# Another order of the expert blocks, and the loop over further blocks and the loads of the sums moved ahead of the last down products

## The chip, the cores and the metric

The kernel runs on one core of one Trainium2 chip. The metric is the device time of one execution in microseconds (us). Three timed executions of the kernel before gave 1248.77, 1251.58 and 1253.98 us; the median, 1251.58 us, is the time that counts.

## The reference, cut to what matters

One transformer block. A mixer (a gated delta net and a gated linear recurrence, both in two directions, over 256 context and 1024 latent tokens) and a first norm come first; the change does not touch them. What follows is a mixture of experts over the 1024 latent tokens h:

```python
combine = jnp.einsum('tk,tke->te', top_w, jax.nn.one_hot(expert_id, N_EXPERTS))   # 2 of 32 experts for each token
a = jnp.einsum('td,edf->tef', h, w_gate[sl])      # 1024 -> 256
b = jnp.einsum('td,edf->tef', h, w_up[sl])
part = jnp.einsum('tef,efd->td', jax.nn.silu(a) * b * combine[:, sl, None], w_down[sl])   # 256 -> 1024
...
x = post_norm(DEEP_ALPHA * x + gt2_l * f_l, ln_g[l, 1], ln_b[l, 1])
```

All 32 experts are used, so the weights of all of them are read: 2 MB of gate and up weights and 1 MB of down weights for each, in f32.

## The kernel before, in words

**Blocks.** The 2048 pairs of token and expert are packed into 22 blocks of 128 rows. Experts are ranked by how many tokens chose them, and `SHAPE` says which ranks share a block: blocks 0 to 2 belong to rank 0, blocks 3 to 9 to ranks 1 to 7, and blocks 10 to 21 hold pieces of several ranks (21 holds ranks 28 to 31, 20 holds ranks 21, 22, 26 and 27, the others two ranks each). `ORDER` lists the blocks in the order in which they are computed. Below, a block is called by its place in that order, so place 0 is block 21 in both kernels.

**A block.** `gather` (L1496, GpSimd) fetches its 128 token rows from DRAM, `transpose` (L1505, 8 TensorE transposes) turns them, `up` (L1529) multiplies them by the gate and up weights, contraction tile by contraction tile: tiles 0 to 3 need the first of the two loads of an expert's up weights, tiles 4 to 7 the second. Then come the SiLU (L1531, ScalarE) and the product (L1532, VectorE), `turn` (L1538, two transposes, and the copy L1540), and `down` (L1553 and the scaling L1554). `scatter` (L1565, GpSimd) adds the 128 rows to the sums `acc` in DRAM. In a block of several ranks a token can stand twice; `alike` and `join` (L1576, L1588) add such rows up first, on TensorE. The last two places (`LATE`) are not scattered: their products stay in SBUF (`keep`, L1556 and L1557) and TensorE adds them at the end.

**Weights.** `ahead` hands out 18 places of 8 KB per partition (`UNITS`); one expert takes two for up and one for down, so six experts fit. It issues loads on SyncE's queue (L1396 up, L1402 down) in the order in which `ORDER` first uses the experts. A load waits until its place is free and, by `behind` with `DEPTH` 2, until the load before last has landed, so at most two are under way. The `ahead` call that follows the first three gathers passes `after`: the first load that this call issues also waits for that gather.

**Order of the work.** A scheduler lays out each engine's instructions at compile time, from priorities in program order and a timing model. So instructions can stand on an engine in another order than in the code. The loop over further blocks (L1660, for pairs that found no room in the 22 blocks) has a count read at run time. For the inputs here the count is zero and the body is skipped, but each engine must still reach the loop, wait there for everything that the other engines and the DMA queues were given ahead of it, and branch past it.

**The end.** After the loop come the loads of ln_g and ln_b (L1697, L1698) and of the eight tiles of sums `xs` (L1705, 0.5 MB each). `total` then adds, tile by tile, the kept products of the last two places (L1723) and, for six of the eight tiles, the sums by an identity matrix (L1725); for tiles 0 and 3 VectorE adds them (L1743). The norm (ScalarE L1747 and L1748, a chain on GpSimd, VectorE L1751 and L1752) and the stores (L1755) close the kernel.

Of the kernel before, what the change touches and what calls it, by code (L numbers as in the profile page):

```python
# [9 lines left out]
F32 = mybir.dt.float32  # L10
F32R = mybir.dt.float32r
I32 = mybir.dt.int32
# [18 lines left out]
         + [[(2, 64), (20, 64)], [(11, 64), (19, 64)], [(12, 64), (18, 64)], [(14, 64), (17, 64)], [(15, 64), (16, 64)]]  # L31
         + [[(21, 32), (22, 32), (26, 32), (27, 32)], [(r, 32) for r in range(28, 32)]])

ORDER = [21, 4, 15, 5, 19, 16, 1, 11, 17, 0, 18, 2, 20, 3, 6, 12, 10, 8, 7, 13, 14, 9]


def plan():
# [52 lines left out]
def hybrid_block(ctx, tc, x, c, ctx_in, c_ctx, w_ada, b_ada, w_in, conv_qkv_w, dn_a_log, dn_dt_bias, dn_onorm_w,  # L90
# [1181 lines left out]
    def split(slot, n, name, s0, T_=T_, ge=None):  # L1272

        ge = T_([P, 2, n, 32], name + "ge") if ge is None else ge
        sk, ski, hii = T_([P, 2, n], name + "sk"), T_([P, 2, n], name + "ski", I32), T_([P, 2, n], name + "hii", I32)
        slo, shi = T_([P, 2, n], name + "slo"), T_([P, 2, n], name + "shi")
        V.tensor_tensor(ge, slot[:, None].to_broadcast([P, 2, n, 32]), Of[:, :, s0:s0 + n], op=ALU.mult)
        V.tensor_reduce(sk, ge, axis=AX.X, op=ALU.add)
        V.tensor_copy(ski, sk)
        V.tensor_scalar(hii, ski, 7, None, op0=ALU.arith_shift_right)  # L1280
        V.tensor_copy(shi, hii)
        V.tensor_scalar(ski, ski, 127, None, op0=ALU.bitwise_and)
        V.tensor_copy(slo, ski)
        return slo, shi
# [93 lines left out]
    def place(i, shape):  # L1378

        return pool_of(i).tile(shape, F32, name=f"u{i}", tag=f"u{i}")  # L1380
# [9 lines left out]
    def load_w(e, places, after=None):  # L1390

        ws = []
        src = w_up[bass.ds(e, 1)].rearrange("o p (k f) -> p (o k) f", k=KT)
        for q, i in enumerate(places):
            w = place(i, [P, 4, 512])
            behind(nc.sync.dma_start(w, src[:, 4 * q:4 * q + 4, :]), None if q else after)  # L1396
            ws.append(w)
        return ws

    def load_d(e, places, after=None):  # L1400
        w = place(places[0], [P, 2, D])
        behind(nc.sync.dma_start(w, w_down[bass.ds(e, 1)].rearrange("o p (k f) -> p (o k) f", k=2)), after)  # L1402
        return w
# [10 lines left out]
    def ahead(done, done_d, after=None):  # L1414

        for h, k in zip(held, (done, done_d)):
            for r in sorted(h, key=lambda r: uses[r][-1]):
                if uses[r][-1] <= k:
                    free.extend(h.pop(r))
        if not known:  # L1420
            return
        for r in uses:
            for ws, h, load, n in ((W, held[0], load_w, 2), (Wd, held[1], load_d, 1)):
                if r not in ws:
                    if len(free) < n or any(pool_of(i) is None for i in free[:n]):
# [171 lines left out]
    def count_over():  # L1597
# [8 lines left out]
        V.tensor_scalar(ov, ov, 128.0, 128.0 * NBLK, op0=ALU.mult, op1=ALU.add)  # L1606
        V.tensor_tensor(ov, ov, kv[:, 3, :], op=ALU.subtract)

    blocks, keeps = [], []

    def make(i):
# [7 lines left out]

    for i in range(3):  # L1620
        make(i)
    ahead(-1, -1, after=blocks[2].got)
    blocks[0].transpose()
    for i in range(NBLK + 1):
        if i < NBLK:
# [16 lines left out]
            blocks[i - 1].join()  # L1642
        if i == 2:
            count_over()


    osm = sb.tile([P, D], F32, name="osm", tag="xg1")
    used = [0]

    def O_(shape, name, dt=F32):  # L1650
        n = int(np.prod(shape[1:]))
        o = osm[0:shape[0], used[0]:used[0] + n]
        used[0] += n
        o = o if dt == F32 else o.bitcast(dt)
        return o if len(shape) == 2 else o.rearrange("p (a b) -> p a b", b=shape[-1]) if len(shape) == 3 else o.rearrange("p (a b c) -> p a b c", b=shape[2], c=shape[3])

    nov = nc.values_load(novi[0:1, 0:1], min_val=0, max_val=48)
    jb = O_([P, 1], "jb")
    V.memset(jb, 0.0)
    with tc.For_i(0, nov, 1):  # L1660
        jn = O_([P, 1], "jn")
        V.tensor_scalar_add(jn, jb, float(NBLK))
        osp = sb.tile([P, 4, 8, 32], F32, name="osp", tag="xg2")
        oslot, oge = osp[:, 0], osp[:, 1]
        V.tensor_tensor(oge, pos, bc(kv[:, 3, :], 8), op=ALU.is_lt)
        V.tensor_tensor(oslot, pos, bc(ov, 8), op=ALU.add)
        V.scalar_tensor_tensor(oslot, oge, BIG, oslot, op0=ALU.mult, op1=ALU.add)
        oslo, oshi = split(oslot, 8, "ov", 0, O_, osp[:, 2:4])
        bv = O_([P, 2, 8, 2], "obv")
        V.tensor_scalar(oge[:, 0:2, 0:8], oshi, jn, None, op0=ALU.is_equal)  # L1670
        for i in range(2):
            V.tensor_tensor(bv[:, :, :, i], oge[:, 0:2, 0:8], valw[:, i], op=ALU.mult)
        pt = psm.tile([P, 512], F32, name="ptab", tag="ptab")
        for k in range(2):
            alo = sb.tile([P, 8, P], F32, name="xT", tag="xT", bufs=2)
            V.tensor_tensor(alo, io128[:, None, :].to_broadcast([P, 8, P]), oslo[:, k, :, None].to_broadcast([P, 8, P]), op=ALU.is_equal)
            for s in range(8):
                nc.tensor.matmul(pt[:, 0:2], alo[:, s, :], bv[:, k, s, :], start=k == s == 0, stop=k == 1 and s == 7)
        ori, ow = rows_of(pt, 1, "ob")
        le = O_([1, 32], "le")  # L1680
        V.tensor_scalar(le, oin[0:1, :], jb[0:1, :], None, op0=ALU.is_le)
        ef = O_([1, 1], "ef")
        V.tensor_reduce(ef, le, axis=AX.X, op=ALU.add)
        ei = O_([1, 1], "ei", I32)
        V.tensor_copy(ei, ef)
        V.tensor_scalar_add(jb, jb, 1.0)
        e = nc.sync.value_load(ei[0:1, 0:1], min_val=0, max_val=31)
        one = Block(0, [(0, 0, P)], ori, ori, ow)
        one.gather()
        one.transpose()  # L1690
        one.up([load_w(e, (0, 1))])
        one.turn()
        one.down([load_d(e, (2,))])
# [100 lines left out]
```

## Time and profile before

| what | value |
|---|---|
| median of 3 timed runs | 1251.58 us (1248.77 to 1253.98) |
| profiled execution: own time, span | 1239.28 us, 1237.5 us |
| TensorE busy, share of the span | 1122.5 us, 91% |
| mean granted TensorE clock | 0.936 |
| DMA moved | 250.65 MB, mean 203 GB/s |
| loads of expert weights | 96 of 1 MB, the first issued at 805.2 us |
| first up products / last down products / end of the span | 883.4 / 1195.5 / 1237.5 us |

A page of the profile gives the busy time of each engine, the span in 40 slices with TensorE's granted clock and the DMA engines' busy share, the groups of instructions, and the DMA issues. The trace answers finer questions: busy time in any window, an engine's instructions in order of time, and what ended an engine's idle time.

### The profile page before, as it was taken

What the parts mean: (1) busy time and instruction counts of PE and PEld (TensorE: products, weight loads), DVE (VectorE), ACT (ScalarE), POOL (GpSimd) and SP (SyncE); (2) the same over time, 40 slices, a digit from 0 to 9 for tenths busy, and PEclk for the clock granted to TensorE, in tenths of its full rate; (3) what the DMA queues carried; (4) which work ended last, traced back from release to release, by engine and by line L of the source; (5) the groups of instructions that cost most, each with busy time, mean ns of one, the idle gap of its engine ahead of it and who ended that gap; (6) DMA issues with size and microseconds to landing.
All of it is one profiled execution on the core that took longest, in us unless ns stands there. A gap on an engine that the chain in (4) does not pass through costs nothing. (4 is left out here: it accounts for less than half of the span.)

```text
span 1237.5 us, 18636 instructions
## 1 busy us (share of the span) xinstructions
PE 1122.5 (91%) x6828; PEld 712.1 (58%) x6828; DVE 689.3 (56%) x1676; ACT 432.7 (35%) x776; POOL 397.0 (32%) x507
## 2 busy tenths in 40 slices
PE   5799998998999989987899999887699998899985
PEld 2357776776867767655677776666343333234343
DVE  3727569568595785785535867756323223123337
ACT  0534513324231544892221345534112222112213
POOL 1511405214243142342860057563112212111106
PEclk7799999898999999988899999986699999899988
DMA  9503453563545423005888355498799999999956
GB/s 335 179 24 121 146 135 111 140 177 109 150 124 155 113 79 85 1 35 184 263 288 252 133 166 185 154 329 300 264 330 317 338 345 342 340 315 336 309 197 195
DMA packets 145605, 250.65 MB, mean 203 GB/s; under 512 B 35627, under 2 KB 97255, under 8 KB 133224
## 3 DMA queue, kind: packets, MB, share of 16 engines
q1 hardware_dynamic: 132688, 215.94, 52.6%
q0 software_dynamic: 6048, 16.01, 5.3%
q10 hardware_dynamic: 6776, 17.49, 3.7%
q8 instruction: 54, 0.88, 0.3%
q14 instruction: 39, 0.32, 0.1%
HBM read 205.34 MB, written 50.09 MB: 206 GB/s over the span
## 5 line engine op out<-in xcount | busy, mean ns | idle before, releaser
L405 PE MATMUL pj<-hhi,whi 128*128 128x512 f32 (+1 forms) x480 | 189.0, 394 | 4.9 <-ACT s L441 2.8
L406 PE MATMUL pj<-hlo,whi 128*128 128x512 f32 (+1 forms) x480 | 185.8, 387 | 0.0
L407 PE MATMUL pj<-hhi,wlo 128*128 128x512 f32 (+1 forms) x480 | 184.6, 385 | 0.0
L1529 PE MATMUL pu<-u,xT 128*32 128x512 f32 (+2 forms) x768 | 172.5, 624 | 5.5 <-DMA u<-in_w_up_dram 5.0
L405 PEld LDWEIGHTS pj<-hhi,whi 128*128 128x128 f32 x480 | 92.8, 193 | 50.2 <-issue 19.1
L1529 PEld LDWEIGHTS pu<-u,xT 128*32 128x32 f32 (+2 forms) x768 | 54.2, 136 | 92.9 <-issue 78.1
L407 PEld LDWEIGHTS pj<-hhi,wlo 128*128 128x128 f32 x480 | 92.6, 193 | 20.9 <-issue 5.7
L406 PEld LDWEIGHTS pj<-hlo,whi 128*128 128x128 f32 x480 | 92.9, 194 | 19.3 <-issue 5.3
L401 POOL TENSOR_TENSOR wlo<-wraw,whi 128x1024 fp32r<-128x1024 f32 x21 | 53.5, 2546 | 154.2 <-ACT whi L400 117.8
L1553 PE MATMUL py<-u,hT 128*32 128x512 f32 (+2 forms) x384 | 83.6, 614 | 2.0 <-ACT hT L1540 2.0
L1496 POOL DMA_INDIRECT xg<-h2d,tbri x22 | 22.9, 1041 | 170.0 <-PE pf L1505 129.3
L621 DVE TENSOR_TENSOR s<-s,s 80x31 f32<-80x31 f32 (+15 forms) x124 | 65.1, 525 | 19.6 <-DMA s<-ad 10.1
L436 DVE SCALAR_TENSOR_TENSOR cv<-pj,par,cv 128x504 f32<-128x504 f32 (+3 forms) x96 | 63.9, 669 | 11.1 <-ACT cv L424 10.0
L1509 ACT ACTIVATE xT<-pf,mod 128x128 f32<-128x128 f32 x88 | 34.2, 456 | 93.9 <-PE pf L1505 93.7
L1532 DVE TENSOR_TENSOR hid<-hid,pu 128x256 f32<-128x256 f32 x22 | 9.3, 421 | 95.5 <-ACT hid L1531 95.5
L623 DVE TENSOR_TENSOR s<-s,s 80x31 f32<-80x31 f32 (+15 forms) x124 | 58.5, 472 | 2.3
L1554 DVE SCALAR_TENSOR_TENSOR y<-py,tbw,gt 128x512 f32<-128x512 f32 x44 | 33.0, 750 | 47.8 <-PE py L1553 47.5
L405 PE MATMUL pf<-whi,yh 128*128 128x512 f32 x128 | 55.2, 431 | 3.7 <-ACT yh L1029 2.6
L1553 PEld LDWEIGHTS py<-u,hT 128*32 128x32 f32 (+2 forms) x384 | 27.1, 135 | 50.3 <-issue 46.4
L407 PE MATMUL pf<-whi,yl 128*128 128x512 f32 x128 | 53.3, 416 | 0.6 <-POOL yl L1030 0.6
L406 PE MATMUL pf<-wlo,yh 128*128 128x512 f32 x128 | 53.1, 415 | 0.0
L1174 DVE SCALAR_TENSOR_TENSOR S<-S,dec,p 128x128 f32<-128x128 f32 x144 | 40.6, 341 | 21.2 <-PE p L1167 20.9
(514 smaller groups left out, 2147.0 us busy)
## 6 DMA issues: line engine op xcount, KB each, us to landing
u<-in_w_up_dram SPq DMA_DIRECT2D x64, 1024.0 KB, 7.4
u<-in_w_down_dram SPq DMA_DIRECT2D x32, 1024.0 KB, 8.7
st<-sp SPq DMA_DIRECT2D x52, 384.0 KB, 4.9
wraw<-in_w_ada_dram SPq DMA_DIRECT2D x32, 512.0 KB, 3.8
wraw<-in_w_in_dram SPq DMA_DIRECT2D x24, 512.0 KB, 5.9
wada<-in_w_ada_dram SPq DMA_DIRECT2D x4, 2048.0 KB, 8.2
sp<-t SPq DMA_DIRECT2D x12, 512.0 KB, 4.3
wor<-in_w_out_dram SPq DMA_DIRECT2D x8, 512.0 KB, 5.9
```

The source lines that it names most:

```text
L401: (nc.vector if i in PA["LOV"] else nc.gpsimd).tensor_tensor(lo, raw, hi.bitcast(F32), op=ALU.subtract)
L405: nc.tensor.matmul(o, lh, rh, start=start, stop=False)
L406: nc.tensor.matmul(o, lh, rl, start=False, stop=False)
L407: nc.tensor.matmul(o, ll, rh, start=False, stop=stop)
L436: nc.vector.scalar_tensor_tensor(yo, xi, w(j), yo, op0=ALU.mult, op1=ALU.add)
L621: nc.vector.tensor_tensor(t_, sa[:, j + 1:32, j:j + 1].to_broadcast([80, n, j + 1]), T[:, j:j + 1, 0:j + 1].to_broadcast([80, n, j + 1]), ...
L623: nc.vector.tensor_tensor(T[:, j + 1:32, 0:j + 1], T[:, j + 1:32, 0:j + 1], t_, op=ALU.subtract)
L1174: nc.vector.scalar_tensor_tensor(s2[:, d, :], S[h][:, d, :], gl[:, (t + d) % 2, m, d, h:h + 1], p3[d][:, h, :], op0=ALU.mult, op1=ALU.add)
L1509: nc.scalar.activation(self.xT[:, i, 0:u], pt[:, k * P:k * P + u], AF.Identity, bias=mod2[:, 0, i:i + 1], scale=mod2[:, 1, i:i + 1])
L1529: turn(nc.tensor.matmul(pu[o:o + n, :], self.xT[:, k, o:o + n], ws[r][k // 4][:, k % 4, :], start=k == 0, stop=k == KT - 1))
L1553: turn(nc.tensor.matmul(py[o:o + n, :], self.hT[:, f, o:o + n], ws[r][:, f, qs], start=f == 0, stop=f == 1))
L1554: nc.vector.scalar_tensor_tensor(y[0:u, qs], py[0:u, :], self.weights[0:u], gt2[0:u, qs], op0=ALU.mult, op1=ALU.mult)
```

## The change

Three edits. `ORDER` is another permutation; place 0 is the same block, the last two places are now blocks 12 and 19. The loop, and behind it the loads of ln_g, ln_b and of the sums, move into a function `further`, called in the turn of place 21 after its `up`, after the `down` of place 20 and after the `turn` of place 21, that is ahead of the `down` of place 21; the loads go to places taken from the free list. And the `after` of the `ahead` call is the first gather where it was the third.

```diff
-ORDER = [21, 4, 15, 5, 19, 16, 1, 11, 17, 0, 18, 2, 20, 3, 6, 12, 10, 8, 7, 13, 14, 9]
+ORDER = [21, 14, 17, 18, 4, 9, 2, 15, 1, 16, 3, 10, 0, 5, 20, 11, 7, 13, 8, 6, 12, 19]
...
+    def further():
+        assert all(p in free for p in (8, 9, 11))
+        room = [p for p in free if p not in (8, 9, 11)]
...
+        nov = nc.values_load(novi[0:1, 0:1], min_val=0, max_val=48)
...
+        with tc.For_i(0, nov, 1):
...
+            one.up([load_w(e, room[5:7])])
+            one.turn()
+            one.down([load_d(e, room[7:8])])
+        gb = place(room[4], [P, 2, D])
+        lg1, lb1 = gb[:, 0, :], gb[:, 1, :]
+        nc.sync.dma_start(lg1, ln_g[0, 1:2, :].to_broadcast([P, D]))
+        nc.sync.dma_start(lb1, ln_b[0, 1:2, :].to_broadcast([P, D]))
+        xs = []
+        for i in range(4):
+            x2 = place(room[i], [P, 2, D])
+            for q in range(2):
+                t = 2 * i + q
+                xs.append(x2[:, q, :])
+                nc.sync.dma_start(xs[t], acc[t * P:(t + 1) * P, :])
+        return lg1, lb1, xs
...
-    ahead(-1, -1, after=blocks[2].got)
+    ahead(-1, -1, after=blocks[0].got)
...
         if i == 2:
             count_over()
...
-    nov = nc.values_load(novi[0:1, 0:1], min_val=0, max_val=48)
...
-    with tc.For_i(0, nov, 1):
...
+        if i == NBLK - 1:
+            final = further()
 
     gb = place(3, [P, 2, D])
-    lg1, lb1 = gb[:, 0, :], gb[:, 1, :]
-    nc.sync.dma_start(lg1, ln_g[0, 1:2, :].to_broadcast([P, D]))
-    nc.sync.dma_start(lb1, ln_b[0, 1:2, :].to_broadcast([P, D]))
-    xs = []
-    for i in range(4):
-        x2 = place(4 + i, [P, 2, D])
-        for q in range(2):
-            t = 2 * i + q
-            xs.append(x2[:, q, :])
-            nc.sync.dma_start(xs[t], acc[t * P:(t + 1) * P, :])
+
+    lg1, lb1, xs = final
```

## Rows read from the trace of the kernel before

**Rows 1.** The page: busy share of the DMA engines in 40 slices.

```profile
DMA  9503453563545423005888355498799999999956
```

**Rows 2.** Windows: us; busy PE, PEld, DVE, ACT, POOL; granted clock, DMA share, GB/s.

```profile
881.50:1195.50 314.00, 300.25 (x1438) 116.38 (x1438) 88.76 (x237) 64.72 (x157) 51.28 (x39) 0.97 0.92 315
...
1020.00:1040.00 20.00, 20.00 (x76) 8.79 (x72) 7.15 (x19) 4.41 (x12) 3.66 (x3) 1.00 1.01 354
...
878.00:882.00 4.00, 0.48 (x3) 0.49 (x4) 0.04 (x1) 0.00 (x0) 2.72 (x3) 0.50 0.33 74
...
1178.00:1180.00 2.00, 2.00 (x12) 0.39 (x8) 0.41 (x3) 0.00 (x0) 0.00 (x0) 0.50 0.79 332
...
1184.00:1186.00 2.00, 2.00 (x6) 0.84 (x5) 0.72 (x2) 0.62 (x1) 0.00 (x0) 1.00 0.03 12
```

**Rows 3.** Groups of instructions from 880 to 1200 us: the joins' products.

```profile
L1588 PE MATMUL py<-y,same 128*128 128x512 f32 x44 | 21.0, 593 | 0.0
```

**Rows 4.** TensorE in order of time: start, us, what, count, idle before it.

```profile
883.41 9.01 PE L1529 MATMUL pu<-u,xT 128*32 128x512 f32 x64
...
907.37 2.80 PE L1529 MATMUL pu<-u,xT 128*64 128x512 f32 x12
...
1055.47 10.00 PE L1529 MATMUL pu<-u,xT 128*32 128x512 f32 x58 [4.65 <-DMA u<-in_w_up_dram]
...
1176.70 0.44 PE L1538 MATMUL pf<-ident,hid 128*128 128x128 f32 x2 [1.91 <-DVE hid L1532]
1177.65 5.23 PE L1553 MATMUL py<-u,hT 128*32 128x512 f32 x32 [0.52 <-ACT hT L1540]
1182.81 7.13 PE L1529 MATMUL pu<-u,xT 128*128 128x512 f32 x16
...
1191.83 3.70 PE L1553 MATMUL py<-u,hT 128*128 128x512 f32 x8 [0.52 <-ACT hT L1540]
1197.67 2.70 PE L1723 MATMUL pn<-u,u 128*128 128x512 f32 x6 [2.14 <-DVE u L1557]
```

**Rows 5.** SyncE's queue in order of time: 6th, 7th, 10th, 23rd, 32nd expert, the sums.

```profile
885.23 0.33 SPq L1402 DMA_DIRECT2D u<-in_w_down_dram  x1
889.00 4.04 SPq L1396 DMA_DIRECT2D u<-in_w_up_dram  x2
...
919.34 3.91 SPq L1396 DMA_DIRECT2D u<-in_w_up_dram  x2
...
1069.64 2.95 SPq L1396 DMA_DIRECT2D u<-in_w_up_dram  x2
...
1170.39 3.84 SPq L1396 DMA_DIRECT2D u<-in_w_up_dram  x2
1179.84 0.33 SPq L1402 DMA_DIRECT2D u<-in_w_down_dram  x1
1195.86 0.81 SPq L1705 DMA_DIRECT2D u<-acc  x2
```

**Rows 6.** Waits of SyncE's queue: us in total, times, longest.

```profile
SPq L1402 <- DMA xg<-h2d,tbri: 11.2, 1, 11.2
```

**Rows 7.** The loop's line, TensorE's waits there: ns min/median/max, first and last start.

```profile
L1660 PEldq EVENT_SEMAPHORE  x13: 51/51/51, 1195.6 to 1197.3; - x13
```

**Rows 8.** VectorE and ScalarE in order of time: a kept product scaled, then copied.

```profile
1193.85 0.75 DVE L1554 SCALAR_TENSOR_TENSOR y<-py,tbw,gt 128x512 f32<-128x512 f32 x1 [3.03 <-PE py L1553]
...
1196.14 0.62 ACT L1556 CAST u<-y 128x512 fp32r<-128x512 f32 x1 [4.36 <-PEq L1660]
```

**Rows 9.** VectorE at the end: its first addition of sums, its last operation.

```profile
1203.25 1.23 DVE L1743 SCALAR_TENSOR_TENSOR u<-pn,u 128x1024 f32<-128x1024 f32 x1 [3.73 <-PE pn L1723]
...
1231.54 1.28 DVE L1752 SCALAR_TENSOR_TENSOR u<-u,rs,u 128x1024 f32<-128x1024 f32 x1 [0.72 <-POOL rs L159]
```

**Rows 10.** The page's DMA issues: count, KB each, median us to landing.

```profile
u<-in_w_up_dram SPq DMA_DIRECT2D x64, 1024.0 KB, 7.4
```

**Rows 11.** The scatters' line L1565: time from issue to landing.

```profile
DMA to landing us min/median/max: 8.8/10.5/13.3
```

More of the change, by code (lines that the diff above doesn't have):

```diff
@@ L1607, in count_over, with O_ @@
         V.tensor_tensor(ov, ov, kv[:, 3, :], op=ALU.subtract)
+    def further():
+        assert all(p in free for p in (8, 9, 11))
+        room = [p for p in free if p not in (8, 9, 11)]
+        osm = sb.tile([P, D], F32, name="osm", tag="xg1")
+        used = [0]
+        def O_(shape, name, dt=F32):
+            n = int(np.prod(shape[1:]))
+            o = osm[0:shape[0], used[0]:used[0] + n]
+            used[0] += n
+            o = o if dt == F32 else o.bitcast(dt)
+            return o if len(shape) == 2 else o.rearrange("p (a b) -> p a b", b=shape[-1]) if len(shape) == 3 else o.rearrange("p (a b c) -> p a b c", b=shape[2], c=shape[3])
+        nov = nc.values_load(novi[0:1, 0:1], min_val=0, max_val=48)
+        jb = O_([P, 1], "jb")
+        V.memset(jb, 0.0)
+        with tc.For_i(0, nov, 1):
+            jn = O_([P, 1], "jn")
+            V.tensor_scalar_add(jn, jb, float(NBLK))
+            osp = sb.tile([P, 4, 8, 32], F32, name="osp", tag="xg2")
+            oslot, oge = osp[:, 0], osp[:, 1]
+            V.tensor_tensor(oge, pos, bc(kv[:, 3, :], 8), op=ALU.is_lt)
+            V.tensor_tensor(oslot, pos, bc(ov, 8), op=ALU.add)
+            V.scalar_tensor_tensor(oslot, oge, BIG, oslot, op0=ALU.mult, op1=ALU.add)
+            oslo, oshi = split(oslot, 8, "ov", 0, O_, osp[:, 2:4])
+            bv = O_([P, 2, 8, 2], "obv")
+            V.tensor_scalar(oge[:, 0:2, 0:8], oshi, jn, None, op0=ALU.is_equal)
+            for i in range(2):
+                V.tensor_tensor(bv[:, :, :, i], oge[:, 0:2, 0:8], valw[:, i], op=ALU.mult)
+            pt = psm.tile([P, 512], F32, name="ptab", tag="ptab")
+            for k in range(2):
+                alo = sb.tile([P, 8, P], F32, name="xT", tag="xT", bufs=2)
+                V.tensor_tensor(alo, io128[:, None, :].to_broadcast([P, 8, P]), oslo[:, k, :, None].to_broadcast([P, 8, P]), op=ALU.is_equal)
+                for s in range(8):
+                    nc.tensor.matmul(pt[:, 0:2], alo[:, s, :], bv[:, k, s, :], start=k == s == 0, stop=k == 1 and s == 7)
+            ori, ow = rows_of(pt, 1, "ob")
+            le = O_([1, 32], "le")
+            V.tensor_scalar(le, oin[0:1, :], jb[0:1, :], None, op0=ALU.is_le)
+            ef = O_([1, 1], "ef")
+            V.tensor_reduce(ef, le, axis=AX.X, op=ALU.add)
+            ei = O_([1, 1], "ei", I32)
+            V.tensor_copy(ei, ef)
+            V.tensor_scalar_add(jb, jb, 1.0)
+            e = nc.sync.value_load(ei[0:1, 0:1], min_val=0, max_val=31)
+            one = Block(0, [(0, 0, P)], ori, ori, ow)
+            one.gather()
+            one.transpose()
+            one.up([load_w(e, room[5:7])])
[13 more added lines that the diff above has]
+        return lg1, lb1, xs
@@ L1644, in hybrid_block @@
             count_over()
[L1647 to L1655, printed above, removed]
-    nov = nc.values_load(novi[0:1, 0:1], min_val=0, max_val=48)
@@ L1658, in hybrid_block @@
-    jb = O_([P, 1], "jb")
-    V.memset(jb, 0.0)
-    with tc.For_i(0, nov, 1):
[L1661 to L1693, printed above, removed]
```

## Prediction

> **What bounds the kernel now.** I read the page's slices first. The change touches only what lies after 880 us, and there the DMA engines are 80 to 99% busy in nearly every slice up to 1180 [rows 1]. Next come the windows. From 881.5 to 1195.5, the 22 blocks, TensorE is busy 300.3 of 314.0 us and the DMA engines 0.92 of the time; in a full stretch (1020 to 1040) their share is 1.01 at 354 GB/s [rows 2]. So both are close to full, and the question is which waits for which. TensorE's order of time answers it. At place 12 of the old order, the block of four experts, TensorE waits 4.65 us for up weights and then needs 10.0 us for 58 products, where place 0 needs 9.01 for 64 although it begins at half clock [rows 4]. Almost all other idle time is the SiLU chain near the end (1.91 and 0.52 us) [rows 4].
>
> The loads set the pace. Up weights of the 7th expert are issued at 889.0 and of the 32nd at 1170.4 [rows 5]: 281.4 us for 25 experts, 11.3 us each, with gathers and scatters in between. The last load goes at 1179.84, and the DMA share is 0.03 from 1184 on [rows 2, 5]. From there to 1195.86, when the first sums are asked for [rows 5], the DMA engines stand still. What stands behind the last weight is serial: up products of place 21 (1182.81, 7.13 us), its SiLU chain, its down products at 1191.83 (3.70 us), the loop, `total` from 1197.67 [rows 4]. VectorE's first addition of sums starts at 1203.25, 7.4 us after that tile's load was issued at 1195.86; its last operation ends at 1232.82 [rows 5, 9].
>
> **The order, step by step.** It removes no load and no product. What changes is how many experts must have arrived when a place begins. By `SHAPE`, the old order needs 4, 5, 6, 7, 9, 11 experts at places 0 to 5, 17 at place 10, 21 at place 12, 31 at place 20 and 32 at place 21. The new one needs 4, 6, 8, 10, 11, 12 at places 0 to 5, 19 at place 13, 23 at place 14, 30 at place 20, 32 at place 21.
>
> Place lengths: busy time without the joins is (300.3 - 21.0)/22 = 12.7 us a place, a join adds 21.0/11 = 1.9 [rows 2, 3]. Place 0 is the same and place 1 needs what has long come, so place 2 still starts near 907.4 [rows 4], and place 3 at 922.0. It needs the 10th expert: loads issued at 919.3 and 922.9 land about 7.4 us later, 926.7 and 930.3 [rows 5, 10]. First half then, second half from 930.3: some 5 us lost. Places 3 to 13 have four joins, 11 x 12.7 + 4 x 1.9 = 147.3, so place 14 starts near 1074; the 23rd expert (1069.6 and 1072.3, plus 7.4) is there at 1077 and 1079.7: 3 us lost. Three more joins lie before place 21, which is ready for weights at 1077 + 7 x 12.7 + 3 x 1.9 = 1172, or 1175 with the down products of place 20 ahead of its up, as now. So TensorE loses about 8 us to waits, as before, but in small pieces and early, and reaches the last block before its weights: the first half of the 32nd expert is there by 1179.84, because the next load but one waits for it [rows 5]. Places 20 and 21 are both of several ranks now, so one join fewer is done (1.9 us); that hides in the wait.
>
> So the up products of the last block run from 1179.8 rather than 1182.8, and end at 1186.9 rather than 1189.9 (the second half, issued at 1173.9, is there at 1181.3, in time). Gain 3.0 us; bounds: 0, if TensorE again arrives late, and 5.0 (1181.3 plus a half of 3.6 us), if the first half is done while the second still comes.
>
> **The first wait.** The down weights of the sixth expert stood 11.2 us at the head of SyncE's queue for a gather [rows 6], and went at 885.23; the up products of place 0 begin at 883.41 [rows 4] and need the first gather and some transposes before them, so that gather is there near 881.5 and the load can go 3.7 us earlier, into a stretch that is idle now (share 0.33 from 878 to 882) [rows 2]. The next load waits for a place that the up products of place 0 free, at 889.0 in either kernel [rows 4, 5]; so most is lost again. It competes with gathers 2 and 3, wanted only after place 0. Bounds 0 and 3.7 us; I take 0.5, since 889.0 is given by TensorE. It moves the whole feed: up products end at 1186.4, 3.5 us sooner.
>
> **The loop and the loads.** Moved past the last down products, the loop costs what it costs now, at another place. Every engine waits there for all the others and for landed DMAs; TensorE goes through 13 waits from 1195.6 to 1197.3 [rows 7] and issues at 1197.67, 2.1 us after its last product. Before, that ran beside the scaling of the kept products. Now it stands between up and down of place 21, where only the chain of SiLU, product, turn and copy (1.9 us from 1189.94 to 1191.83) can run beside it. With the turn ahead of the loop: 0.95 + 0.44 + 2.1 = 3.5 us; behind it: 2.1 + 0.44 + 0.6 = 3.1. Bounds of the addition: 1.2 and 2.1; I take 1.6. Down starts at 1189.9. Held behind the loop are ScalarE's and VectorE's kept copies, SyncE's ten loads, and nothing on GpSimd until the norm.
>
> The clock: after 1.91 and 0.52 us idle around the turn of place 20, the granted clock is 0.50, the 1.2 GHz level, and 32 down products take 5.23 us [rows 2, 4]; around place 21 with 1.4 us idle it stayed at full and took 3.70. The new gap has 3.1 us idle, so I charge 1.5 us, all of it in the first half. Bounds 0 and 1.5. First half done at 1193.3 (1.85 us and the 1.5). Now a half is done near 1193.7, its scaling ends at 1194.60, the copy starts only at 1196.14, released by the loop [rows 8], and `total` at 1197.67; without those 1.5 us it is 2.4 us from half to `total`. So `total` starts at 1195.7, 2.0 earlier.
>
> The sums: SyncE leaves the loop when the last engine is there, with the copy of the turn at 1186.4 + 1.9, so near 1188.5, and the first tile lands 7.4 us later, 1195.9, so it no longer holds VectorE. Six of tile 0's eight products take 2.70 us [rows 4], so it needs about 3.0, and VectorE starts at 1198.7 rather than 1203.25: 4.5 sooner. Bounds at the end of the span: 2.0, if only TensorE's shift counts, and 4.5, if VectorE's does. I take 4.5: VectorE has the last operation and waits only 0.72 us ahead of it [rows 9].
>
> **Sum**: 3.0 + 0.5 - 1.6 - 1.5 + 1.5 (copy's wait) + 2.6 (the sums' landing) = 4.5 us. The profiled execution, 1239.28 us (1.78 beyond its span), would become 1234.8. The median of the runs is 12.3 us above that execution; I carry the difference over: 1251.58 - 4.5 = 1247.1 us. Own range: 2.5 to 7 us, by the clock and the last block.
>
> **Rivals.** (1) The loop stays where it was: the scheduler places it by readiness, as now, where VectorE passes it between two halves of place 21. Then the loads gain nothing, and the order alone gives 3.5 us: 1248.1. If TensorE also arrives late at place 21, 0 to 1 us: about 1251. (2) The feed quickens. From 881.5 to 1184 the DMA engines are idle for 302.5 - 0.92 x 314 = 13.6 us [rows 2]; with early blocks freeing twelve places at once, half could be used, and the end moves by 6 more: 10 us faster, 1241. Against it: loads now wait for loads, not for places. The Trainium skill (DMA: Bandwidth & Descriptors, Anatomy of one DMA) prices a transfer at about 2 us plus its bytes at 436 GB/s; by that an expert would, as an estimate, take 7.2 us with two loads under way, and TensorE would bound the stage. The 11.3 us of rows 5 at full share do not agree. (3) Slower: the loop waits for the last scatter. A scatter lands 8.8 to 13.3 us after issue [rows 11]. Place 19's should go near 1173.5 and land by 1186. If it goes after 1185, SyncE leaves the loop later than the present 1195.7 and the sums come later than now; behind the up products of place 21 it would go near 1191, land at 1202, VectorE start at 1209.8: 6.5 us slower, 1258. Against it: down of place 19 stands two places ahead.
>
> **Chances.** My forecast 0.47, rival (1) 0.27, rival (2) 0.14, rival (3) 0.12. A measurement of this kernel tells a change of about 0.5%, 6.3 us, from none. Faster by more: rival (2) and 0.2 of chance from the upper part of my range, 0.34; slower 0.12; same 0.54. The range goes from rival (2) with a little beyond to part of the way to rival (3): 1240 to 1254.5.
>
> **What would show it.** TensorE waits for up weights at places 3, 14 and 21 and no longer 4.65 us before the four-expert block alone; the last up products end near 1186; L1660 lies before the last L1553, which takes 5.2 us; L1705 is issued near 1188; VectorE's first L1743 near 1199. Wrong, if the last weights land much before or after 1184, or L1705 stays behind the last L1553.

## The result, and the profile after

The changed kernel is slower by a little over half a per cent: its runs have a median of 1253.03 us (20 runs, 1245.24 to 1265.38), against 1246.94 us (1237.37 to 1257.78) for 20 runs of the kernel before beside them. The ratio is 1.0061, with a 95% interval of 1.0038 to 1.0083. (Ratios here leave out runs more than 1.5% above the fastest of their kernel, one of the changed kernel's, five of twelve in e3 and four of twelve in e13 below, so they are not quotients of the medians and come out low for those two.) The two profiled spans differ by 6.4 us, 1237.5 and 1243.9 us, and I split that at marks that both traces have.

TensorE in order of time, after (start, us, what, idle before it):

```profile
1083.71 9.39 PE L1529 MATMUL pu<-u,xT 128*32 128x512 f32 x58 [4.47 <-DMA u<-in_w_up_dram]
...
1185.80 7.14 PE L1529 MATMUL pu<-u,xT 128*64 128x512 f32 x30 [2.73 <-DMA u<-in_w_up_dram]
1193.87 0.44 PE L1538 MATMUL pf<-ident,hid 128*128 128x128 f32 x2 [0.93 <-DVE hid L1532]
1196.81 5.35 PE L1553 MATMUL py<-u,hT 128*64 128x512 f32 x16 [2.50 <-issue]
1202.09 2.60 PE L1733 MATMUL pn<-u,u 128*128 128x512 f32 x10
1204.52 1.02 PE L1735 MATMUL pn<-u,ident 128*128 128x512 f32 x2
1204.98 1.97 PE L1733 MATMUL pn<-u,u 128*128 128x512 f32 x6
1206.79 1.02 PE L1735 MATMUL pn<-u,ident 128*128 128x512 f32 x2
1207.25 2.21 PE L1733 MATMUL pn<-u,u 128*128 128x512 f32 x7
...
1214.69 0.50 PE L1733 MATMUL pn<-u,u 128*128 128x512 f32 x1 [1.43 <-DVE u L1753]
```

The last up products end at 1192.94; before it was 1189.94 [rows 4], so 3.0 us of the loss lie ahead of this mark. From it to the last down products it takes 3.9 us in place of 1.9: the loop now stands there (2.50 us of "issue", idle time for which the profile shows no releaser, where TensorE goes through the loop's waits). From down products to the total it takes 5.3 in place of 5.8 us, and from the total to the end 41.8 in place of 39.8. That is 3.0 + 2.0 - 0.5 + 2.0, less rounding.

SyncE's queue, after:

```profile
880.98 0.33 SPq L1402 DMA_DIRECT2D u<-in_w_down_dram  x1
888.52 3.77 SPq L1396 DMA_DIRECT2D u<-in_w_up_dram  x2
...
1165.35 0.33 SPq L1396 DMA_DIRECT2D u<-in_w_up_dram  x1
1168.39 0.34 SPq L1663 DMA_DIRECT2D u<-in_ln_g_dram  x1
1168.94 0.35 SPq L1396 DMA_DIRECT2D u<-in_w_up_dram  x1
1169.34 0.67 SPq L1664 DMA_DIRECT2D u<-in_ln_b_dram  x1
...
1177.82 4.04 SPq L1396 DMA_DIRECT2D u<-in_w_up_dram  x2
1185.78 0.33 SPq L1402 DMA_DIRECT2D u<-in_w_down_dram  x1
1195.32 4.81 SPq L1671 DMA_DIRECT2D u<-acc  x7
```

The up weights of the 32nd expert are asked for 7.4 us later than before (1170.39) [rows 5], and the loads of ln_g and ln_b, which stood behind the loop, now stand ahead of them: the scheduler moved them past the loop, since nothing in it concerns them. The sums go at 1195.32, half a microsecond before their old time, although the loop is no longer behind the down products.

VectorE's first addition of sums and its last operation, after:

```profile
1209.26 1.23 DVE L1753 SCALAR_TENSOR_TENSOR u<-pn,u 128x1024 f32<-128x1024 f32 x1 [4.92 <-PE pn L1733]
...
1237.88 1.28 DVE L1762 SCALAR_TENSOR_TENSOR u<-u,rs,u 128x1024 f32<-128x1024 f32 x1 [0.71 <-POOL rs L159]
```

The first addition comes 7.2 us after the total's start; before it was 5.6 us [rows 4, 9]. It waits for TensorE in both kernels, not for a load. In the rows above TensorE does 23 products and four additions of sums by about the time that VectorE starts, though tile 0 needs eight products. From VectorE's first addition to the end of the span it takes 34.2 us before and 34.6 after, so most of the 2.0 us lost from the total to the end is this later start.

Windows, after: the last down products, the total's start (granted clock, DMA share and GB/s last):

```profile
1196.80:1202.10 5.30, 5.29 (x17) 1.48 (x17) 1.44 (x2) 0.62 (x1) 0.00 (x0) 0.68 0.88 322
1202.10:1207.60 5.50, 5.50 (x23) 3.86 (x21) 1.44 (x2) 0.62 (x1) 0.00 (x0) 1.00 1.02 415
```

The pause in the loop costs the clock behind it: after 0.93 and 2.50 us of idle time the granted clock is 0.68 in the down products, between its two levels (1.2 and 2.4 GHz), then full speed in the total. Before it was the other way round, as the same windows of the kernel before show:

```profile
1191.80:1195.50 3.70, 3.67 (x8) 1.44 (x8) 0.75 (x1) 0.00 (x0) 0.00 (x0) 1.00 0.00 0
1197.70:1203.20 5.50, 5.50 (x17) 4.39 (x18) 1.14 (x2) 0.62 (x1) 0.00 (x0) 0.69 0.95 340
```

### The profile page after: what moved, and what is told of

It reads as the page before. It is cut to its first block, busy times and chain, and to the rows that moved or that the text cites. A ratio compares the mean times of both kernels' runs of the same rounds, so it can differ in the third digit from the quotient of the medians.

```text
span 1243.9 us, 18598 instructions
## 1 busy us (share of the span) xinstructions
PE 1123.5 (90%) x6822; PEld 713.3 (57%) x6822; DVE 686.9 (55%) x1670; ACT 431.0 (35%) x774; POOL 398.4 (32%) x507
## 5 line engine op out<-in xcount | busy, mean ns | idle before, releaser
L1529 PE MATMUL pu<-u,xT 128*32 128x512 f32 (+2 forms) x768 | 174.2, 622 | 13.4 <-DMA u<-in_w_up_dram 12.1
L1529 PEld LDWEIGHTS pu<-u,xT 128*32 128x32 f32 (+2 forms) x768 | 55.1, 136 | 104.3 <-issue 79.2
L406 PEld LDWEIGHTS pj<-hlo,whi 128*128 128x128 f32 x480 | 93.0, 194 | 19.2 <-issue 5.3
L1553 PEld LDWEIGHTS py<-u,hT 128*32 128x32 f32 (+2 forms) x384 | 27.2, 134 | 51.5 <-issue 47.3
L1174 DVE SCALAR_TENSOR_TENSOR S<-S,dec,p 128x128 f32<-128x128 f32 x144 | 40.6, 342 | 20.6 <-PE p L1167 20.3
```

The costliest lines, as they stand in the source:

```text
L406: nc.tensor.matmul(o, lh, rl, start=False, stop=False)
L1174: nc.vector.scalar_tensor_tensor(s2[:, d, :], S[h][:, d, :], gl[:, (t + d) % 2, m, d, h:h + 1], p3[d][:, h, :], op0=ALU.mult, op1=ALU.add)
L1529: turn(nc.tensor.matmul(pu[o:o + n, :], self.xT[:, k, o:o + n], ws[r][k // 4][:, k % 4, :], start=k == 0, stop=k == KT - 1))
L1553: turn(nc.tensor.matmul(py[o:o + n, :], self.hT[:, f, o:o + n], ws[r][:, f, qs], start=f == 0, stop=f == 1))
```

## The experiments: what they are read by

Executions of one kernel lie some 20 us apart here, so the interval of a ratio is 0.2 to 0.6% to either side. There is one trace of each kernel. The trace tells more, if each stage is measured from its own start. "Stage" is from the first up products (L1529) to the end of the last ones, "end" from there to the end of the span, "total" from the total's first product to the end of the span, and "V" from the total's first product to VectorE's first addition of sums. "Order" is that of the blocks, "loop" its place, and "tiles" says whether the total's tiles were kept in turn on TensorE. Where the loop's place is new, the loads of the sums and of the norm's rows moved with it.

| run | order | loop | tiles | stage | end | total | V | ratio (95%) |
|---|---|---|---|---|---|---|---|---|
| before | old | old | | 306.5 | 47.6 | 39.8 | 5.6 | 1 |
| after | new | new | | 310.2 | 51.0 | 41.8 | 7.2 | 1.0061 (1.0038 to 1.0083) |
| e1 | new | old | | 315.0 | 56.6 | 48.9 | 10.4 | 1.0119 (1.0058 to 1.0180) |
| e2 | old | new | | 313.8 | 50.8 | 42.1 | 7.5 | 1.0051 (1.0016 to 1.0085) |
| e3 | old | old | | 309.3 | 47.2 | 39.4 | 5.6 | 0.9990 (0.9944 to 1.0036) |
| e4 | new | new | | 315.5 | 51.6 | 40.5 | 5.6 | 1.0043 (1.0011 to 1.0075) |
| e5 | new | old | | 310.1 | 48.3 | 40.6 | 5.6 | 1.0046 (1.0018 to 1.0075) |
| e6 | old | none | | 307.0 | 49.2 | 44.2 | 8.8 | 1.0015 (0.9981 to 1.0049) |
| e7 | old | old | | 313.1 | 65.1 | 39.5 | 3.6 | 1.0162 (1.0122 to 1.0201) |
| e8 | new | none | | 305.4 | 47.3 | 41.8 | 5.8 | 1.0021 (0.9987 to 1.0054) |
| e9 | old | old | | 308.0 | 51.2 | 43.5 | 8.7 | 1.0034 (1.0002 to 1.0067) |
| e10 | old | none | | 309.7 | 47.9 | 42.9 | 7.5 | 0.9988 (0.9960 to 1.0017) |
| e11 | new | new | | 314.2 | 51.0 | 41.9 | 7.2 | 1.0056 (1.0026 to 1.0086) |
| e12 | new | old | | 310.3 | 48.3 | 40.6 | 5.6 | 1.0022 (0.9992 to 1.0051) |
| e13 | new | new | in turn | 315.7 | 48.9 | 38.8 | 2.9 | 0.9976 (0.9943 to 1.0009) |
| e14 | old | old | in turn | 307.6 | 46.9 | 39.2 | 3.1 | 0.9966 (0.9936 to 0.9996) |
| e15 | old | none | in turn | 313.9 | 45.2 | 40.2 | 3.7 | 0.9970 (0.9935 to 1.0004) |
| e16 | old | old | in turn | 312.3 | 48.2 | 40.5 | 3.0 | 1.0037 (1.0008 to 1.0066) |
| e17 | new | old | in turn | 315.6 | 46.6 | 38.9 | 2.9 | 1.0040 (1.0006 to 1.0073) |
| e18 | old | new | in turn | 312.8 | 47.9 | 39.2 | 3.3 | 1.0019 (0.9981 to 1.0058) |

## The three parts alone (e1, e2, e3), and the norm's rows (e4)

```diff
 e1, from before:
+ORDER = [21, 14, 17, 18, 4, 9, 2, 15, 1, 16, 3, 10, 0, 5, 20, 11, 7, 13, 8, 6, 12, 19]
 e2, from after: the old ORDER, and
+    ahead(-1, -1, after=blocks[2].got)
 e3, from before:
+    ahead(-1, -1, after=blocks[0].got)
 e4, from after, in further():
+        last = loads[-1]
...
+        later(nc.sync.dma_start(lg1, ...), last)
+        later(nc.sync.dma_start(lb1, ...), last)
```

`later(s, o)` is the kernel's own helper, also behind `behind`: s is placed after o.

> The kernel before with the new order alone; loop, sums and gather wait as before. Theory F (the profile after: the last up weights are issued 7.4 us later than before, 3 us of it by the two norm loads that now run ahead of them, the rest by the order): the order alone makes 3 to 4 us, ratio 1.003, and its last down weights are issued near 1183 instead of 1179.8. Theory L (all of it comes from the move of the loop and what rides on it): ratio 1.000 or a little below, last down weights near 1180. Theory O (the order is all of it): ratio 1.006.

> The old order and the old gather wait, with the loop and the loads of sums ahead of the last down products. Theory F: the gap from the last up products to the last down products grows by 2 us, the down products go at half clock (5.3 us instead of 3.7), the norm's stage is 1.9 us longer, and the sums gain little: ratio 1.003. Theory L: ratio 1.006. Theory O, and the prediction's step: ratio 1.000 to 0.998.

> The kernel before with the weights behind the first gather only. All theories: the sixth expert's down weights go 4 us earlier (881 instead of 885), the next load at 889 as before, ratio 0.999 to 1.000.

> The changed kernel with the loads of ln_g and ln_b made to wait for the last weights, so they no longer run ahead of the 32nd expert's. Theory F: the last weights land 3 us sooner than in the changed kernel; against the kernel before the ratio falls from 1.006 to about 1.0035. Theory O: no change, 1.006, because other things than the feed end the stage.

**e1** is the slowest of the four, and not by the feed alone: its stage is 8.5 us longer than before, and 9 us are lost behind the total's start. The sums and the norm's rows on SyncE's queue in e1:

```profile
1204.24 3.30 SPq L1705 DMA_DIRECT2D u<-acc  x3
1207.59 0.43 SPq L1697 DMA_DIRECT2D u<-in_ln_g_dram  x1
1208.06 0.43 SPq L1698 DMA_DIRECT2D u<-in_ln_b_dram  x1
1208.54 2.71 SPq L1705 DMA_DIRECT2D u<-acc  x5
```

VectorE's first addition of sums in e1:

```profile
1216.45 1.23 DVE L1743 SCALAR_TENSOR_TENSOR u<-pn,u 128x1024 f32<-128x1024 f32 x1 [8.81 <-DMA u<-acc]
```

TensorE in e1, behind that addition:

```profile
1217.74 3.62 PE L1723 MATMUL pn<-u,u 128*128 128x512 f32 x8 [5.02 <-DVE u L1743]
```

The eight sums go to fixed places 4 to 7 in the kernel before. The new order frees them at other times, and the scheduler issued three other sums and both rows ahead of tile 0's. Here VectorE does wait for a load. I had not expected that the order reaches this far; in the changed kernel `room`, the free places, hides it.

**e2** shows the same end as the changed kernel (50.8 and 51.0 us) with the old order: the move of the loop and its loads makes it. **e3** changes nothing that can be measured, as predicted (0.9990; the medians, 1251.42 against 1247.60 us, give 1.0031).

**e4** was to take the rows out of the feed. It put a new wait in: `later` between two of SyncE's loads waits for the first to land, and the loop then waits for the rows to land as well. TensorE of e4, the last down products:

```profile
1211.28 5.71 PE L1553 MATMUL py<-u,hT 128*64 128x512 f32 x16 [4.08 <-DMA u<-in_ln_b_dram]
```

So it says nothing of the rows' price; e11 asks again.

## Where the sums go, and what the loop costs (e5 to e8)

```diff
 e5, from e1:
+    room = [p for p in free if p not in (0, 1, 2, 8, 9, 11)]
+    gb = place(room[4], [P, 2, D])
+        x2 = place(room[i], [P, 2, D])
 e6, from before, and e8, from after: the loop's body and its count left out; in e6 room as above
+            last = later(nc.sync.dma_start(xs[t], acc[t * P:(t + 1) * P, :]), last)   # last: loads[-1], then the sum ahead
 e7, from e3: the same line for eight sums ahead of the loop, and in its body
+        for t in range(8):
+            nc.sync.dma_start(xs[t], acc[t * P:(t + 1) * P, :])
```

> The kernel before with the new order of blocks alone, as in the run of the order alone (ratio 1.0119), but the sums and the norm's two rows go into the buffers that came free first, not into buffers 3 to 7. Theory P (the 9 us that the order alone lost behind the total are a late first sum: its buffer was among the last to come free, so its load was issued fourth): total to end 40 to 42 us in place of 48.9, ratio 1.002 to 1.006, what is left being the weights' feed (289 us from the 7th to the 32nd up loads, 281.4 before). Rival Q (the new order itself makes the end late, by the state in which it leaves the engines): total to end stays above 46 us, ratio 1.009 or more.

> The kernel before (old order) without the loop over further blocks, which runs no pass with these inputs; the loads of the sums and of the norm's rows are issued behind the last weight load. Theory A (loop and late sums are all that the change could win at this end): last down products to total 5.8 to about 4.0 us, total to end 39.9 to about 38 us, ratio 0.996 to 0.998. Rival B (the sums' loads now compete with the last weights, or wait for the last scatter): the last up products end later by 1 to 3 us relative to the first, ratio 0.999 to 1.002. It is also one more sample of the old order's feed: 281 to 285 us if the order sets the feed, up to 290 if it varies from run to run.

> The kernel before (old order) with the first wait for one gather, and the sums loaded behind the last weight load and ahead of the loop, which stays where it was and loads them again in each pass (no pass with these inputs). Theory A: the first sum is there when the total starts, total to end 39.9 to about 38 us, loop still between last down products and total (5.8 us), ratio 0.997 to 0.999. Rival C (the loop waits for these loads, or for their last, as for all work ahead of it): last down products to total 7 us or more, nothing won, ratio 0.999 to 1.002.

> The changed kernel without the loop over further blocks (no pass with these inputs), the loads of the sums and of the norm's rows issued behind the last weight load. Theory L (the loop's place between the last transposes and the last down products is what made the change slower): last up products to last down products back from 3.9 to 1.9 us, sums there at the total, ratio to before 0.996 to 1.000. Theory F (the feed under the new order is later as well): the same gain at the end but feed 288 to 293 us and last weights 308 to 314 us after the first up products, ratio 1.001 to 1.004.

**e5** settles e1: V is 5.6 us again, the end 48.3, the ratio 1.0046. Theory P holds, and the places of the sums, with the late first sum, were worth 8.3 us of end.

**e6, e7 and e8** carry the wait of e4 eight times: each sum was issued only when the one ahead of it had landed. In e7 the loop, and everything behind it, waited for that chain. The sums on SyncE's queue in e7:

```profile
1199.32 25.69 SPq L1656 DMA_DIRECT2D u<-acc  x8
```

TensorE in e7, the last down products and the total's start:

```profile
1205.77 3.70 PE L1553 MATMUL py<-u,hT 128*128 128x512 f32 x8 [0.52 <-ACT hT L1540]
1229.50 2.93 PE L1728 MATMUL pn<-u,u 128*128 128x512 f32 x6 [20.03 <-SPq L1674]
```

That is a clean price for rival C: for loads that stand ahead of the loop on SyncE's queue and have not landed, TensorE waits at the loop, here 20 us in place of 2.1. Without the loop (e6, e8) the total starts 5.0 and 5.5 us after the last up products in place of 7.7 (before) and 9.2 (after), so the loop costs TensorE some 2.7 us at its old place and 3.7 at the new one. Theory L is right in that the loop's place costs; but e8 came out at 1.0021, with an interval that takes in 1.000, and e6's total grew to 44.2 us.

## Sums without the chain (e9, e10), rows behind the weights (e11), loop at its old place (e12)

```diff
 e9 to e12: the wait is now on a matmul, self.first, of the last up products
+                    if k == 0 and r == self.pieces[0][0]:      # e11, e12: k == KT // 2, pieces[-1]
+                        self.first = m
 e9, from e3: sums 0 to 3 and both rows ahead of the loop, sums 4 to 7 behind it
+    for t in range(4):
+        later(load_sum(t), up_)                                # up_: blocks[-1].first
 e10, from e6: eight sums and both rows each later(..., up_)
 e11, from after: both rows later(..., blocks[-1].first)
 e12, from e5: after=blocks[0].got, both rows as in e11
```

> The kernel before (old order), first wait for one gather; the sums of tiles 0 to 3 and the norm's two rows are loaded once the last up products start, the loop stays at its old place (it loads the four sums again in a pass; no pass with these inputs), the other four sums follow it. No load waits here for another's landing, as each of the eight did in the run with all sums ahead. Theory A: loop still 1.7 us ahead of the total (last down products to total 5.8 us), first sums there, total to end 39.4 to 39.9 before, now 37 to 38.5, ratio 0.996 to 0.999. Rival C (the loop waits for the loads ahead of it to land, as it waited for the chain of eight): last down products to total 7 to 10 us, ratio 1.000 to 1.004.

> The kernel before (old order) without the loop (no pass with these inputs), sums and norm rows issued once the last up products start, none waiting for another's landing. It bounds what any place of the loop can give. Theory A: last down products to total 5.8 to 3.1 to 3.7 us (the run without the loop had 3.1), total to end 39.9 to 37 to 39 us, ratio 0.995 to 0.998. Rival (the norm stage is bound by VectorE and GpSimd, and gives back what comes earlier): total to end 41 us or more, ratio 0.999 or above.

> The changed kernel, with the loads of the norm's two rows tied to the second half of the last up products, so that they are issued behind all weights and wait for no landing. Theory F (the 1.05 MB ahead of the last weights is 3 us of the loss): last weights 305 to 306 us after the first up products in place of 308.6, end of the up products earlier by 2 to 3 us, last up products to end 51 us as in the changed kernel, ratio 1.002 to 1.005. Rival (the loop's place is the loss, the feed differs from run to run by more than these rows): ratio 1.004 to 1.008 as the changed kernel, 1.0061.

> The changed kernel with the loop and the sums put back behind the last down products: the new order, the first wait for one gather, the sums in the buffers that came free first, the norm's rows behind all weights. Theory L (the loop's place is the loss, 3.4 us between the last up products and the end): last up products to end 47.3 to 48.3 us in place of 51, ratio 0.999 to 1.002. Theory F (the new order's feed is later by itself): the same at the end, but last up products 309 to 314 us after the first, ratio 1.002 to 1.005, no better than the changed kernel with the rows behind the weights.

Theory A falls twice. In **e9** the loop takes what it took (5.8 us from down products to total) and the four sums are there, yet V grows to 8.7 and the total to 43.5 us. In **e10** there is no loop at all, the sums go at 1192.67, 10 us before the total, and the end is 47.9 us, no shorter than before. TensorE of e10 shows the pattern of the changed kernel again:

```profile
1202.81 2.96 PE L1692 MATMUL pn<-u,u 128*128 128x512 f32 x10
1205.61 1.02 PE L1694 MATMUL pn<-u,ident 128*128 128x512 f32 x2
1206.06 1.97 PE L1692 MATMUL pn<-u,u 128*128 128x512 f32 x6
1207.87 1.02 PE L1694 MATMUL pn<-u,ident 128*128 128x512 f32 x2
1208.33 2.21 PE L1692 MATMUL pn<-u,u 128*128 128x512 f32 x7
```

In the kernels whose loads follow the loop in the program (before, e3, e5, e12) V is 5.6 us. With the sums earlier the scheduler mixes the matmuls of the first tiles, V is 7.2 to 8.8 us and the total takes 41.8 to 44.2 us (after, e2, e6, e9, e10, e11). Not in every such kernel: in e4 and e8 V stayed at 5.6 and 5.8; and e8's total took 41.8 us all the same, so V is not all that sets it.

**e12** against **e11** prices the loop's move, with the sums and the total's order of matmuls that come with it: end 48.3 against 51.0 us, ratio 1.0022 against 1.0056 (their intervals overlap). **e11** itself, with the rows behind all weights, is no better than the changed kernel, so no gain is shown from them; its stage was longer (314.2 us), not shorter by 3.

## The total's tiles kept in turn (e13 to e18)

```diff
 in total(), for e13 (from after), e14 (e9), e15 (e10), e16 (before), e17 (e12), e18 (e13, old ORDER):
+                    m = nc.tensor.matmul(pt[:, q, :], oh[:, i, t, :], keeps[i][:, h, qs], ...)
+                    if ended and q == i == h == 0:
+                        later(m, ended[-1])
 ...
+                m = nc.tensor.matmul(pt[:, q, :], ident, xs[t][:, qs], start=False, stop=True)
+        ended.append(m)
```

> The changed kernel; each tile's products of the total start only when those of the tile ahead of it have ended (an order on TensorE alone; nothing else changes). Theory T (the norm stage is 1.9 us longer because the scheduler, with the sums there earlier, put matmuls of tiles 1 and 2 between those of tile 0, so that VectorE's first operation came 7.1 us after the total's start in place of 5.6): first VectorE operation 4 to 5 us after the total's start, total to end 38.5 to 40 us in place of 41.8, ratio 1.003 to 1.006. Rival (the stage is bound by the chain of VectorE and GpSimd behind it, and waits just as long elsewhere): total to end 41 us or more, ratio 1.005 to 1.008.

> The kernel with four sums and the norm's rows loaded ahead of the loop at its old place (old order of blocks, first wait for one gather), and the total's tiles in turn. Theory T: what the early sums can give appears once the tiles keep their order: total to end 43.5 to 37.5 to 39 us (before 39.9), last up products to end 45.5 to 47 us (before 47.6), ratio 0.996 to 1.000: the one kernel with the loop left in that could end ahead of the kernel before. Rival: total to end 40 us or more, ratio 1.000 to 1.004.

> The kernel before without the loop (no pass with these inputs), sums and rows loaded once the last up products start, and the total's tiles in turn: the bound on what the change's second and third part together could give. Theory T: last down products to total 3.1 us, total to end 42.9 to 38 to 39.5 us, last up products to end 43 to 44.5 us (before 47.6), ratio 0.994 to 0.997. Rival: total to end 41 us or more, ratio 0.998 to 1.000.

> The kernel before with the total's tiles in turn, nothing else. If the early sums and not the tiles' order made the run with four sums ahead come out ahead of the kernel before (ratio 0.9966), this one stays at 0.998 to 1.002 with total to end 39 to 41 us, VectorE's first operation waiting for the load of the first sum. If the order of the tiles is the whole of it: total to end 38 to 39 us, ratio 0.995 to 0.998.

> The new order of blocks, the first wait for one gather, the loop at its old place, the norm's rows behind all weights, the total's tiles in turn. With the changed kernel with tiles in turn (0.9976; last up products to end 48.9 us) it tells what the loop's place costs once the tiles' order is fixed. Loop's place still costs 1 to 2 us: last up products to end 46.5 to 48 us here, ratio 0.995 to 0.999. Rival (its early sums now pay for it): 48.5 us or more, ratio 0.998 to 1.001.

> The changed kernel with tiles in turn, but the old order of blocks: with the run of the changed kernel with tiles in turn it tells what the order of blocks does when the end is the same. If the new order costs 2 to 3 us (as the pairs without the tiles in turn had it, between 0 and 4 us): ratio 0.993 to 0.997. If it costs nothing: 0.996 to 1.000. Last up products to end 48 to 49 us in both cases.

TensorE of e13 from the total's start on:

```profile
1212.76 2.08 PE L1734 MATMUL pn<-u,u 128*128 128x512 f32 x7
1215.07 1.43 PE L1734 MATMUL pn<-u,u 128*128 128x512 f32 x5 [0.23 <-DVE u L1557]
1216.34 1.02 PE L1738 MATMUL pn<-u,ident 128*128 128x512 f32 x2
```

VectorE's first addition in e13:

```profile
1215.61 1.22 DVE L1757 SCALAR_TENSOR_TENSOR u<-pn,u 128x1024 f32<-128x1024 f32 x1 [0.59 <-PE pn L1734]
```

**e13** keeps the whole change and fixes only this order: V falls from 7.2 to 2.9 us, the total from 41.8 to 38.8, the end from 51.0 to 48.9. **e18** does the same to e2: 50.8 to 47.9. So Theory T is shown for the norm stage, 3 us of total in both. In e13 the end gains 1 us less than the total, because its down products took 6.32 us at a granted clock of 0.57, in place of 5.35. The ratios moved the same way, from 1.0061 to 0.9976 and from 1.0051 to 1.0019; that of e13 moved by 0.85%, some 10 us, where its trace has 2.1 us. Its medians over all runs, 1251.34 against 1249.86 us, give 1.0012, so I rest nothing on its size.

How little an early start is worth is seen in **e16**: the kernel before with its tiles in turn. VectorE starts 3.0 us after the total, held now by the first sum, and the end comes no earlier (48.2 us). VectorE's first addition of e16:

```profile
1209.36 1.22 DVE L1747 SCALAR_TENSOR_TENSOR u<-pn,u 128x1024 f32<-128x1024 f32 x1 [1.18 <-DMA u<-acc]
```

So of the 2.6 us by which the tiles in turn advance VectorE, the rest of the norm gave all back there. Over all six kernels with tiles in turn the total takes 38.8 to 40.2 us with early sums (e13, e14, e15, e18), and 40.5 and 38.9 with late ones (e16, e17): nothing to tell apart.

**e14** is the only one of the eighteen whose interval lies below 1, that is ahead of the kernel before: 0.9966, interval 0.9936 to 0.9996. Its end is 0.7 us shorter, 0.06%; the other 0.3% no trace shows, and the interval nearly touches 1; of eighteen intervals one may miss by chance. **e15**, without the loop, bounds the idea: end 45.2 us, 2.4 us less than before, 0.2%. **e17** against **e13**, with the same order of blocks and tiles, leaves 2.3 us of end (46.6 and 48.9) for the loop's new place, 1.0 of it because e13's down products were slower than the changed kernel's. Their ratios (1.0040 and 0.9976) say the opposite; the medians over all runs (1.0020 and 1.0012) tell no difference. The same move with the old order, **e16** against e18, costs nothing: end 48.2 and 47.9. So what the loop's place costs once the tiles are in turn is not settled. Nor did e18 price the order of the blocks, as it was to: with 1.0019 it does not lie below e13.

## Why the prediction was wrong, point by point

The sum was -4.5 us; the profiled spans gave +6.4. Two steps make up the difference. The time itself, 1253.03 us, lies inside the range of 1240 to 1254.5, and that is luck: the three runs that gave 1251.58 lay 4.6 us above the median of all twenty (1246.94), and the step went the other way.

**The last up products** (predicted 3.5 us sooner with order and first wait, measured 3.0 later). TensorE did in part as foretold: it waited at place 14 (4.47 us at 1083.71, predicted 3 us up to 1079.7) and reached place 21 ahead of its weights (2.73 us of wait); at place 3, where 5 us were predicted, no wait shows. What failed is "it moves the whole feed", and behind it the assumption that the feed takes 281.4 us in either kernel. It took 289.3 us, from 888.52 to 1177.82, and the last load of all went at 1185.78 in place of 1179.84. That is no property of the new order alone: e2 has the same instructions as the kernel before on every engine up to the norm's two rows, which stand among the loads of the 30th expert, and its feed took 290.5 us. SyncE's queue of e2, the 7th and the 32nd expert:

```profile
900.75 3.77 SPq L1396 DMA_DIRECT2D u<-in_w_up_dram  x2
...
1191.24 4.68 SPq L1396 DMA_DIRECT2D u<-in_w_up_dram  x2
```

And e8, with the new order, had the shortest stage of all, 305.4 us. Over all profiles the feed from the 7th to the 32nd expert took 286.2 us on average for the old order (11 kernels, 281.4 to 290.5) and 289.7 for the new (9 kernels, 282.9 to 293.4), the stage 310.4 and 312.4 us. The differences, 3.5 and 2.0, have a standard error of about 1.5 each: a loss by the order is possible, and not settled. TensorE's idle time in the stage, added up from each trace, is 15.7 us on average for the old order and 19.2 for the new, 3.5 with an error of 1.1. That eats the join that the new order saves (1.9 us), which I let vanish in the wait.

The loop's place divides the profiles no worse than the order does: the six kernels with the loop at its new place, of either order, have a feed of 291.1 us (289.3 to 293.4), the other fourteen 286.3 (281.4 to 292.7), 4.8 apart with an error of 1.1. The whole of it lies ahead of the 28th expert (246.0 and 240.9 us from the 7th to the 28th), where the traces of e2 and of the kernel before show the same instructions in the same order on every engine. So no run shows why, the division was not forecast, and chance is not ruled out. SyncE's queue, the 28th expert, before and after:

```profile
1123.54 5.22 SPq L1396 DMA_DIRECT2D u<-in_w_up_dram  x2
...
1134.65 3.44 SPq L1396 DMA_DIRECT2D u<-in_w_up_dram  x2
```

From the 7th to the 28th expert the changed kernel lost 11.6 us (246.1 against 234.5), and it won 3.7 back up to the 32nd (43.2 against 46.9), where the two rows are loaded. So the rows did not make its feed late: this last stretch takes 45.2 us on average in the four kernels that load them there (after, e2, e13, e18) and 45.3 in the other sixteen.

**VectorE's start** (predicted 3.0 us after the total's start, measured 7.2). I read 7.4 us from the first sum's issue to VectorE's first addition and took it for the load's landing. The row itself named TensorE as the releaser [rows 9], and rightly: in e16, where the load does release it, it comes 4.85 us after the issue at 1204.51. The early sums could therefore not give 2.6 us. They came with a loss of 2.0, the scheduler's order of the total's matmuls having changed with them; and where that order is kept tile by tile, early sums are not told from late ones (e13 to e18).

The other steps held. **The first wait**: the sixth expert's down load went at 880.98 (predicted 3.7 us earlier than 885.23), the next at 888.52, and e3 measures nothing. **The loop**: predicted 1.6 us between up and down products, bounds 1.2 and 2.1; measured 2.0. Rival (1), that it would stay behind, did not happen. **The clock**: predicted 1.5 us in the down products, measured 1.65 (5.35 against 3.70). What I left out is that it is a debt moved: the total then runs at full clock, where before its first products ran at 0.69, over 5.5 us. **The sums' issue**: predicted 2.1 us after the end of the up products, measured 2.4; so it moved with them. **Rival (2)**, a quicker feed, shows in no trace. **Rival (3)**, a wait for the last scatter, did not decide: of SyncE's waits at the loop 1.0 us names the scatter, and the longest, 4.7 us, another engine. SyncE's waits at the loop, after (us in total, times, longest):

```profile
SPq L1627 <- DVEq L1624: 4.7, 1, 4.7
...
SPq L1627 <- DMA u<-in_w_up_dram: 1.1, 1, 1.1
SPq L1627 <- DMA acc<-y,tbri: 1.0, 1, 1.0
```

Of the measured 0.61%, 7.6 us of 1246.94, the end explains 3.4 us (51.0 against 47.6) by the traces: e2 has it with the loop moved alone, e12 loses most of it with the loop put back, and e13 and e18 win 2.1 and 2.9 us of it back by the tiles. The rest, some 4 us with the interval from 1.3 to 6.9, lies ahead of the last up products. A slower feed is where it shows in the traces; whether the order, the loop's place or chance made it slower stays open.

## What to carry to other kernels

Read who released a wait before pricing it: an interval that happens to equal a load's latency is no proof that the load set it, and one run that moves the load alone would have told. The loop moved ahead of the last down products was no cheaper than behind them, and TensorE waited at it for loads that SyncE's queue had been given ahead of it (4.08 us in e4, 20.03 in e7); and where a scheduler lays out the instructions, an edit of one stage can reorder another, so the order of a stage that ends the kernel is better pinned. Compare stages from their own start: the first load of expert weights goes at 805.2 us before and at 816.9 in e2, behind the same instructions.

## What was not expected of the hardware

The feed of weights from the 7th to the 28th expert, by the same instructions on the same queue, took 234.5 us in the kernel before, 238.2 in e3 (first wait aside the same code) and 245.6 in e2, with the DMA engines' share at 0.92 over the stage before and after alike. After TensorE's pause in the loop, whatever came next ran at a lower granted clock: 0.68 in the down products of the changed kernel and of e2, 0.69 in the total's first 5.5 us before, in e12 and in e16, and 0.57 over 6.3 us in e13; without the loop (e8, e10) both stretches ran at 1.00. And a load of 0.5 MB issued first into idle queues released its reader 4.85 us after issue (e16), where the 1 MB loads of the busy stretch took 7.4 us [rows 10].
